# A two-layer hybrid encoder trunk on one Trainium2 core: the phases of a layer laid over one another at their borders, and the attention maximum taken from packed pairs of heads

## The chip, the core and the metric

The kernel runs on one core of one Trainium2 chip. The core has five engines with an instruction queue each: TensorE (PE in the profile, with its weight loads as PEld), VectorE (DVE), ScalarE (ACT), GpSimd (POOL) and SyncE (SP, which here only issues DMAs). Each works its queue in order, and they wait for one another through semaphores. The metric is the device time of one execution in microseconds (us). A kernel's time is the median of its runs; one more execution is taken with the hardware profiler, and its trace is what is read here.

## The reference

There are two layers over x of 1024 tokens by 1024 channels, all float32. In each layer one input projection feeds four token mixers: softmax attention with 8 query heads and 2 key heads of width 64; HGRN2, a gated linear recurrence of 4 heads with 128x128 states, run forward and backward; Mamba-2's SSD with 8 heads, also in both directions; and GLA, linear attention of 4 heads with a gate from a low-rank projection, in both directions. Each branch gets a SiLU gate, the four are joined and go through one output projection, and a LayerNorm ends the layer.

```
for i in range(DEPTH):
    h = einsum('bsd,dn->bsn', x, w_in[i])
    y_a = attention_branch(...)   # softmax(q k^T / 8) v, 128 queries at a time
    y_h = hgrn2_branch(...)       # S_t = diag(g_t) S_{t-1} + k_t v_t^T ; o_t = S_t^T q_t, both ways
    y_s = ssd_branch(...)         # conv, softplus time steps, h_t = exp(dt A) h_{t-1} + dt B x^T, both ways
    y_g = gla_branch(...)         # g = log_sigmoid(low @ w2 + b)/16, the same scan as HGRN2
    out = einsum('bsn,nd->bsd', concat(y_a, y_h, y_s, y_g), w_out[i])
    x = layer_norm(alpha * x + out)
```

"Time steps" and "gates" in the change's name are the softplus of SSD's `dt` and the log-sigmoid of GLA's low-rank projection. Both come from one narrow input tile, `sp`.

## The kernel before

**Tiles.** Activations lie transposed, channels on partitions and tokens along the free axis, in two halves of 512 tokens. Every input and output projection is computed to better than plain fp32r: activation and weight are split into a high and a low fp32r part, and three products are added, `xh*whi`, `xl*whi` and `xh*wlo`. One column tile of 128 output channels takes 48 matmuls of 128x512. ACT casts a weight tile to `whi`, POOL subtracts to get `wlo`. Results that a later phase needs go to DRAM scratch (`hdr`, `yd`) and come back by DMA.

**Phases.** Per layer: (1) q, k, v projections; (2) attention in 8 blocks of 128 queries; (3) HGRN2, head by head; (4) SSD in four tiles of two heads; (5) GLA in two pairs of heads (p = 0, 1), with the output projection beside it; (6) LayerNorm. In an attention block, `a_s` takes each query row's maximum over 1024 keys: per key group 4 matmul pairs into `S` (one head each, with the high and low halves of q stacked to 128 rows), each followed by one DVE reduction. `a_e` computes the transposed scores `ST` with the negative maximum folded in, ACT takes the exponential into `Pt`, and POOL adds up the eight `Pt` for the row sums (`psum`). `a_pv` multiplies by v into `O`, `Z` is the row sum over partitions. HGRN2 and GLA share `tree` (names `lv`, `QP`, `M`, `C`, `T`), which works through seven levels of a gated block decomposition, each with small matmuls on PE and four products on DVE; then come states (`kst`, `P`, `S`) and outputs (`ot`). In GLA `gss` is the sum of squares for the norm, one per output. In SSD, `sP` makes states, `yd` and `yo` the outputs, and DVE combines them (`u`, `ytmp`).

**What sets the order.** The instruction order of every engine is chosen when the program is built, by a planner. Mixer steps are generators, queued with `M(name, ..., needs, lane)` on twelve lanes; projections are generators too, queued with `F(name, ..., after)` as one list of fillers. A generator yields what its next piece waits for: tiles, free PSUM banks (`"A:1"`, `"P:1"`) or free buffers of the two large SBUF pools (`"k2:8"`: eight of 62 buffers of 128x512; `"k4:1"`: one of 8 of 128x1024). `run()` (line 548) keeps a clock for each engine from cost formulas (`Eng.call`, line 262) and always advances the lane whose wait is over first. If that lies more than 100 ns ahead, or if TensorE has fewer columns in the current tick of 3413 ns than `share` asks (`behind`, line 143; `KNOBS` holds the share, 0.5), it advances the filler. A table of dependencies at the end of `layer` (lines 1818 to 1895) fixes which phase may begin after which step: `sp` after HGRN2's last projection and `spp` (gates and time steps, `spec_post`) after its third head; HGRN2's first scan `hn0` after attention's last block; SSD's first group `sgp0` after HGRN2's last head `hm3`; GLA's first loads `gp0` after SSD's fourth tile `sm3`.

**Names the steps below touch.** `NP = (7, 8)` is how many `Pt` and `psum` tiles attention may have alive in each layer. `GL` is how many `k2` buffers have to be free before GLA loads. The SP queue carries every DMA, weights (`wraw`) and reloads alike, in the planner's order.

## Time and profile before

| | us |
|---|---|
| median of 3 runs (2638.04 to 2647.71) | 2640.66 |
| the profiled execution | 2644.85 |
| its span, first to last instruction | 2643.0 |
| PE busy in it | 2481.6 |
| DVE busy | 1588.1 |
| POOL busy | 1227.7 |
| ACT busy | 1092.9 |

The span is the time between the first and the last instruction. The 1.85 us between it and the execution's own time lie around it. "Busy" is the time in which an engine had at least one instruction running. PE's instructions overlap, so a busy PE may still be slowed: "PEclk" is the share of full clock that it was granted, and is 0.97 over the span. Almost all instructions stand under line 299, where a helper records them, so groups are told apart by the names of their tiles (`out<-in`). One fp32 matmul of the program stands in the profile as two records, one fp32r matmul as one.

### The profile page before, as it was taken

The page shows a single profiled execution, that of the slowest core. Times are in us where ns is not written, and L with a number is a line of the kernel's source. Part 1 is how long each engine was busy: PE and PEld are TensorE (multiplying, and loading weights), DVE is VectorE, ACT ScalarE, POOL GpSimd, SP SyncE. Part 2 cuts the span into 40 slices and gives each one's busy share as a digit, 9 for nine tenths or more (in the row PEclk, how much of TensorE's full clock was granted, in tenths as well). Part 3 has the DMA queues.
Part 4 walks back from the last instruction along what each step waited for, and adds up shares of the span by engine and source line. Part 5 has one row for each costly group of instructions (what it writes and reads, how often), then busy time and mean ns, then how long its engine had stood idle before and what let it go on. Part 6 is the DMA issues. An engine that isn't in the chain of part 4 may idle for free. (4 is left out here: it accounts for less than half of the span.)

```text
span 2643.0 us, 46508 instructions
## 1 busy us (share of the span) xinstructions
PE 2481.6 (94%) x18352; PEld 1855.2 (70%) x18352; DVE 1588.1 (60%) x2895; ACT 1092.9 (41%) x2100; POOL 1227.7 (46%) x932
## 2 busy tenths in 40 slices
PE   8999899999989997889989999999999999988996
PEld 6855457777877886667777655577777787866675
DVE  2574520565489778863555745206664898868737
ACT  4445453332464433334344444533334543433342
POOL 3556663223335446423554566642223454564334
PEclk9999999999989998989999999999999899999998
DMA  6311112011137447622343111120111365676232
GB/s 210 100 48 52 36 43 66 33 53 49 46 112 252 148 148 256 218 71 89 100 162 112 64 38 48 51 68 29 57 41 46 131 237 152 189 262 203 79 104 100
DMA packets 170173, 284.38 MB, mean 108 GB/s; under 512 B 17780, under 2 KB 43380, under 8 KB 169956
## 3 DMA queue, kind: packets, MB, share of 16 engines
q1 hardware_dynamic: 169956, 281.41, 32.5%
q8 instruction: 145, 2.38, 0.4%
q14 instruction: 72, 0.59, 0.1%
HBM read 205.39 MB, written 75.96 MB: 106 GB/s over the span
## 5 line engine op out<-in xcount | busy, mean ns | idle before, releaser
L299 POOL TENSOR_TENSOR wlo<-wraw,whi 128x512 fp32r<-128x512 f32 x372 | 509.9, 1391 | 585.3 <-ACT whi L299 528.7
L299 PE MATMUL proj<-xh,whi 128*128 128x512 f32 x1056 | 429.4, 407 | 4.7 <-DVE u L299 4.7
L299 PE MATMUL proj<-xl,whi 128*128 128x512 f32 x1056 | 415.1, 393 | 0.0
L299 PE MATMUL projh<-xh,whi 128*128 128x512 f32 x704 | 287.8, 409 | 10.4 <-ACT whi L299 9.6
L299 POOL TENSOR_TENSOR psum<-psum,Pt 128x1024 f32<-128x1024 f32 x96 | 228.6, 2381 | 128.2 <-ACT Pt L299 123.1
L299 ACT CAST whi<-wraw 128x512 fp32r<-128x512 f32 x372 | 216.6, 623 | 165.0 <-DMA wraw<-in_wt 63.7
L299 PE MATMUL proj<-xh,wlo 128*128 128x512 f32 x1056 | 281.0, 400 | 0.0
L299 PE MATMUL projh<-xl,whi 128*128 128x512 f32 x704 | 280.2, 398 | 0.3 <-DVE xl L299 0.3
L299 PEld LDWEIGHTS proj<-xh,whi 128*128 128x128 f32 x1056 | 199.6, 189 | 49.1 <-ACT ga L299 5.5
L299 PE MATMUL oproj<-mxh,whi 128*128 128x512 f32 x512 | 217.8, 425 | 15.9 <-ACT whi L299 9.2
L299 PEld LDWEIGHTS proj<-xl,whi 128*128 128x128 f32 x1056 | 200.2, 190 | 37.2
L299 PEld LDWEIGHTS proj<-xh,wlo 128*128 128x128 f32 x1056 | 192.6, 188 | 41.3 <-issue 2.1
L299 ACT ACTIVATE Pt<-ST 128x512 f32<-128x512 f32 x256 | 151.1, 597 | 135.6 <-PE ST L299 133.8
L299 PE MATMUL oproj<-mxl,whi 128*128 128x512 f32 x512 | 206.2, 403 | 0.0
L299 PE MATMUL projh<-xh,wlo 128*128 128x512 f32 x704 | 193.9, 398 | 0.0
L299 DVE TENSOR_REDUCE mx<-S 128x1 f32<-128x1024 f32 x128 | 151.9, 1218 | 53.5 <-PE S L299 52.4
L299 DVE TENSOR_TENSOR QP<-QP,T 128x512 f32<-128x512 f32 x168 | 144.7, 861 | 48.4 <-PE lv L299 47.5
L299 PEld LDWEIGHTS projh<-xh,whi 128*128 128x128 f32 x704 | 134.8, 192 | 54.9 <-issue 13.4
L299 ACT COPY M<-C 128x256 f32<-128x256 f32 x168 | 69.4, 415 | 241.2 <-DVE C L299 241.2
L299 PE MATMUL oproj<-mxh,wlo 128*128 128x512 f32 x512 | 152.7, 412 | 4.1 <-POOL wlo L299 4.1
L299 PEld LDWEIGHTS projh<-xl,whi 128*128 128x128 f32 x704 | 134.9, 192 | 27.5 <-DVE xl L299 1.5
L299 PEld LDWEIGHTS projh<-xh,wlo 128*128 128x128 f32 x704 | 129.0, 189 | 35.3 <-issue 9.7
(241 smaller groups left out, 4602.1 us busy)
## 6 DMA issues: line engine op xcount, KB each, us to landing
wraw<-in_wt SPq DMA_DIRECT2D x244, 256.0 KB
wraw<-in_wo SPq DMA_DIRECT2D x128, 256.0 KB
hdr<-zs SPq DMA_DIRECT2D x64, 256.0 KB
zs<-hdr SPq DMA_DIRECT2D x64, 256.0 KB
bc<-dr SPq DMA_DIRECT2D x64, 256.0 KB
yld<-yd SPq DMA_DIRECT2D x56, 256.0 KB
hdr<-sp SPq DMA_DIRECT2D x40, 256.0 KB
yd<-o SPq DMA_DIRECT2D x40, 256.0 KB
```

The lines of the kernel that those rows point to most:

```text
L299: return real(*args, **kw)
```

## The change

The dependency table and the planner's knobs change, and with them the order on every engine:

- **Gates and time steps first.** `sp` becomes a filler right after the q, k, v tiles, and `spp` needs only it (and twelve free `k2` buffers).
- **HGRN2's first head.** Its projection may start after attention's block 4 (`aP{H0}`, H0 = 4) in place of block 6, its scan no longer needs attention's end but two free `k4` buffers. From block 4 on attention may keep only NQ = 4 `Pt`/`psum` tiles alive.
- **SSD's and GLA's starts.** `sgp0` needs HGRN2's third head in place of its fourth; `sgp1` needs SSD's `sw1` in place of `sm0`, for which `CB` is kept apart from `Cc` and `Bt`. GLA's first loads need SSD's third tile (`sm2`) and the last input projection in place of the fourth tile; its second loads need `sm3`.
- **Knobs.** `share` goes from 0.5 to 1.0; POOL's cost formula is a little higher; `a_pv` gets a lane of its own.
- **Attention's maximum.** `a_qprep` also makes a copy `qp` of q with 64 channels a head, and transposes it so that one `Q2` chunk holds two heads on partitions 0 to 63 and 64 to 127. `a_s` then issues two matmuls of 64 rows, one per head, for one half of the keys, into the two halves of `S`. The reduction gives two columns at once, and one more DVE operation joins the two halves. As many matmuls and reductions are issued as before; per block there are 4 more transposes and 2 more ACT copies.
- **Row sums.** The additions into `psum` go from POOL to DVE.

```diff
+H0, NQ = 4, 4
-KNOBS = ((None, 100, 0.5),)
+KNOBS = ((None, 100, 1.0),)
-                cost = 155 + 2.09 * n + (120 if fn == "tensor_copy" else 0)
+                cost = 160 + 2.17 * n + (120 if fn == "tensor_copy" else 0)
@@ h_mix, second_half
+                yield ["k4:2"]
@@ spec_post
-            yield [spec, w2]
+            yield [spec, w2, "k2:12"]
@@ a_qprep
+                    qp = k2("qp", F32R)
+                    ac.copy(qp, qr)
+                    yield [qp, "A:1"]
+                    pt = transpose4(lambda c: qp[:, ck(c)], "qpT", F32R)
+                    Q2 = k2("Q2", F32R)
+                    ac.copy(Q2, pt.bitcast(F32))
@@ a_s
-                for c in range(4):
-                    yield [QT, "P:1"]
-                    S = bigps("S")
-                    for sh in range(2):
-                        mm(hs(S, sh), QT[:, ck(c)], KK[g * 2][sh], True, True)
-                    yield [S]
-                    ve.tensor_reduce(out=mx[:, c:c + 1], in_=S, axis=AX.X, op=ALU.max)
+                for c in range(2):
+                    for sh in range(2):
+                        yield [Q2, "P:1"]
+                        S = bigps("S")
+                        for e in range(2):
+                            r = slice(e * 64, e * 64 + 64)
+                            mm(hs(S, e), Q2[r, ck(2 * g + c)], KK[g * 2][sh][r], True, True)
+                        yield [S]
+                        ve.tensor_reduce(out=mx[:, sh * 4 + 2 * c:sh * 4 + 2 * c + 2], in_=AV(S, 0, [[HALF, 2], [1, HALF]]), axis=AX.X, op=ALU.max)
+                tt(ve, mx[:, 0:4], mx[:, 0:4], mx[:, 4:8], ALU.max)
@@ a_e
-                    yield [lambda: live[0] < NP[li], "k4:1"]
+                    yield [lambda: live[0] < (NP[li] if ti < H0 else NQ), "k4:1"]
-                        tt(gp, acc_s, acc_s, P, ALU.add)
+                        tt(ve, acc_s, acc_s, P, ALU.add)
@@ the table of dependencies
+        F(f"sp{li}", spec_proj, after=x1 + [f"set{li}"], ws=[wsrc("sp")])
+        M(f"spp{li}", spec_post, needs=[f"sp{li}"], lane=3)
-            F(f"hp{li}{h}", h_proj(h), after=... [f"set{li}", f"aP{li}6" if h == 0 else f"aP{li}7"],
+            F(f"hp{li}{h}", h_proj(h), after=... [f"set{li}", f"aP{li}{H0}" if h == 0 else f"aP{li}7"],
-            M(f"hn{li}{h}", a, needs=[f"hp{li}{h}", f"aP{li}7"])
+            M(f"hn{li}{h}", a, needs=[f"hp{li}{h}"])
-        F(f"sp{li}", spec_proj, after=[f"hp{li}3"], ws=[wsrc("sp")])
-        M(f"spp{li}", spec_post, needs=[f"sp{li}", f"hm{li}2"], lane=3)
-            M(f"sgp{li}{g}", ... (exps if g == 0 else [f"sm{li}0"]), lane=3)
+            M(f"sgp{li}{g}", ... ([f"hm{li}2"] if g == 0 else [f"sw{li}1"]), lane=3)
-            M(f"gp{li}{p}", g_load(p), needs=names + ([f"sm{li}3"] if p == 0 else [f"gn{li}0"]), lane=8)
+            M(f"gp{li}{p}", g_load(p), needs=names + ([xlast, f"sm{li}2"] if p == 0 else [f"sm{li}3"]), lane=8)
```

What the planner makes of it, at three places.

**PE, layer 0, about the third attention block.** `S` is the score tile for the maximum, `ST` the transposed scores, `projh` a filler projection. Before:

```order
L299 MATMUL S<-KK,QT 128x512 x2
L299 MATMUL ST<-QT,KK 128x512
L299 MATMUL ST<-QM,KK 128x512
L299 MATMUL S<-KK,QT 128x512 x2
L299 MATMUL qhT<-ident,qhl 128x128 x4
L299 MATMUL projh<-xh,whi 128x512
L299 MATMUL projh<-xl,whi 128x512
```

and now:

```order
L300 MATMUL S<-KK,Q_1949 128x512 x2
L300 MATMUL ST<-QT,KK 128x512
L300 MATMUL ST<-QM,KK 128x512
L300 MATMUL projh<-xh,whi 128x512
L300 MATMUL projh<-xl,whi 128x512
L300 MATMUL projh<-xh,wlo 128x512 x4
L300 MATMUL qpT<-ident,qp 128x128 x4
```

The `S` matmuls still come two by two, and full-size matmuls still stand on both sides of each pair; `S` now reads 64 rows in each, and `qpT`, the transposes of the packed q, are new.

**SP, layer 0, where the input projections end and the output projection begins.** `wraw<-in_wo` are the output projection's weights, `yld` its input, `M`, `q`, `T` and `V` GLA's first loads, `off` a load of SSD's fourth tile. Before:

```order
L299 DMA off<-dro 64x512 x4
L299 DMA hdr<-u 128x512
L299 DMA zs<-hdr 128x512
L299 DMA wraw<-in_wo 128x512 x2
L299 DMA xr<-in_xT 128x512 x2
L299 DMA wraw<-in_wo 128x512 x2
L299 DMA xr<-in_xT 128x512
L299 DMA hdr<-u 128x512
L299 DMA zs<-hdr 128x512
L299 DMA M<-hdr 128x512
L299 DMA q<-hdr 128x512
L299 DMA T_9326<-hdr 128x512 x2
```

and now:

```order
L300 DMA yld<-yd 128x512 x4
L300 DMA M<-hdr 128x512
L300 DMA q<-hdr 128x512
L300 DMA T_9169<-hdr 128x512 x2
L300 DMA wraw<-in_wo 128x512 x4
L300 DMA hdr<-zs 128x512 x2
L300 DMA off<-dro 64x512 x4
L300 DMA V<-hdr 128x512 x2
```

Before, GLA's first loads stood behind the first eight weight loads of the output projection. Now four of them stand ahead of its first weight load, and ahead of the fourth tile's last `off`. In layer 1 the first loads stand behind the weights as before.

**DVE, layer 0, the same border.** `QP<-q,T` is the first product of GLA's tree, `u` and `ytmp` are SSD's fourth tile, second half, `acc` the sums of the output projection. Before:

```order
L299 SCALAR_TENSOR_TENSOR S<-S,dec,sP 128x64 x6
L299 SCALAR_TENSOR_TENSOR acc<-xr,oproj 128x512 x2
L299 SCALAR_TENSOR_TENSOR u<-u,pk,yd 128x512
L299 TENSOR_TENSOR ytmp<-yo,off 128x512
L299 TENSOR_TENSOR ytmp<-yo,off 128x384
L299 SCALAR_TENSOR_TENSOR acc<-xr,oproj 128x512 x4
L299 TENSOR_TENSOR QP<-q,T_9352 128x1024
L299 TENSOR_TENSOR QP<-q,T_9326 128x1024
```

and now:

```order
L300 SCALAR_TENSOR_TENSOR S<-S,dec,sP 128x64 x6
L300 TENSOR_TENSOR QP<-q,T_9384 128x1024
L300 TENSOR_TENSOR QP<-q,T_9169 128x1024
L300 SCALAR_TENSOR_TENSOR acc<-xr,oproj 128x512 x2
L300 TENSOR_TENSOR near<-lv,imask 128x128 x2
L300 TENSOR_TENSOR M<-M,T_9384 128x128x2
L300 TENSOR_TENSOR QP<-QP,T_9384 128x256x2
L300 TENSOR_TENSOR C<-M,T_9384 128x128x2
L300 TENSOR_TENSOR T<-T_9384 128x512
L300 COPY_PREDICATED near<-masks,lv 128x128 x2
L300 SCALAR_TENSOR_TENSOR acc<-xr,oproj 128x512 x2
L300 SCALAR_TENSOR_TENSOR u<-u,pk,yd 128x512
```

GLA's tree now begins ahead of the fourth tile's last outputs, by one `u`, two `ytmp` and some `acc`.

Counted over the whole order of PE, as numbers of matmuls of the program:

| | before, layer 0 | before, layer 1 | now, layer 0 | now, layer 1 |
|---|---|---|---|---|
| projection matmuls between the first `S` and the last `Z` of attention | 368 | 410 | 490 | 500 |
| `oproj` matmuls between GLA's first `lv` and its last `gss` | 324 | 392 | 398 | 496 |
| `oproj` matmuls behind GLA's last `gss` | 358 | 242 | 304 | 200 |

The changes of tile form between neighbouring matmuls (full, 64 or 32 columns, 64 rows) number 663 before and 929 now. `gk` (16 matmuls a layer) and `colT` (16), which are the gates and time steps, stand beside HGRN2's last head and behind it before, and now beside attention's first two blocks. In layer 1 the first `proj` of HGRN2's first head stands behind the last `Z` of attention before and now; in layer 0 it stood behind it, and now stands ahead of it.

More of the change, by code (lines that the diff above doesn't have):

```diff
@@ L1265, in gen @@
                     yield None
-                sd["g", g] = (Cc, CB, Bt)
+                sd["g", g] = (Cc, Bt)
+                sd["cb", g] = CB
             return gen
@@ L1290, in gen @@
                 colA, dr = sd["colA"], sd["dr"]
-                CB = sd["g", n // 2][1]
+                CB = sd["cb", n // 2] if n % 2 == 0 else sd.pop(("cb", n // 2))
                 def rows(hf, e):
@@ L1336, in gen @@
                 colB, dro, dec = (sd[k] for k in ("colB", "dro", "dec"))
-                Cc, CB, Bt = sd["g", n // 2] if n % 2 == 0 else sd.pop(("g", n // 2))
-                del CB
+                Cc, Bt = sd["g", n // 2] if n % 2 == 0 else sd.pop(("g", n // 2))
                 X, xt = sd.pop(("x", n))
@@ L1582, in gen @@
                     tt(ve, q8, q8, AV(rq, 0, [[1, 8], [0, 64]]), ALU.mult)
+                    qp = k2("qp", F32R)
[4 more added lines that the diff above has]
+                    ac.copy(Q2, pt.bitcast(F32))
+                    del qp
                     for g in range(2):
@@ L1592, in gen @@
                         ac.copy(QT, pt.bitcast(F32))
-                        qts[ti, g] = (QT, qhl)
+                        qts[ti, g] = (QT, Q2, qhl)
             return gen
@@ L1600, in gen @@
                 yield [lambda: (ti, g) in qts]
-                QT, qhl = qts.pop((ti, g))
-                mx = mt("c8", [128, 4], name="mx")
-                for c in range(4):
-                    yield [QT, "P:1"]
-                    S = bigps("S")
-                    for sh in range(2):
-                        mm(hs(S, sh), QT[:, ck(c)], KK[g * 2][sh], True, True)
-                    yield [S]
-                    ve.tensor_reduce(out=mx[:, c:c + 1], in_=S, axis=AX.X, op=ALU.max)
-                    drop(S)
+                QT, Q2, qhl = qts.pop((ti, g))
+                mx = mt("c8", [128, 8], name="mx")
+                for c in range(2):
+                    for sh in range(2):
+                        yield [Q2, "P:1"]
[5 more added lines that the diff above has]
+                        ve.tensor_reduce(out=mx[:, sh * 4 + 2 * c:sh * 4 + 2 * c + 2], in_=AV(S, 0, [[HALF, 2], [1, HALF]]), axis=AX.X, op=ALU.max)
+                        drop(S)
+                del Q2
+                tt(ve, mx[:, 0:4], mx[:, 0:4], mx[:, 4:8], ALU.max)
+                mx = mx[:, 0:4]
                 mh = AV(qhl, 64, [[128, 4]])
@@ L1643, in gen @@
                         acc_s = k4("psum")
-                        tt(gp, acc_s, pts[ti, 0], P, ALU.add)
+                        tt(ve, acc_s, pts[ti, 0], P, ALU.add)
                         live[0] += 1
                     elif st:
-                        tt(gp, acc_s, acc_s, P, ALU.add)
+                        tt(ve, acc_s, acc_s, P, ALU.add)
                 sums[ti] = acc_s
@@ L1835, in layer @@
             M(f"ae{li}{ti}", a_e(ti), needs=[f"akv{li}a", f"akv{li}b"], lane=6)
[L1836 removed]
+            M(f"aP{li}{ti}", a_pv(ti), needs=[f"akv{li}a", f"akv{li}b", f"az{li}3"], lane=11)
         for h in range(4):
[L1839 removed]
+            F(f"hp{li}{h}", h_proj(h), after=[f"hm{li}{h - 2}"] if h > 1 else [f"set{li}", f"aP{li}{H0}" if h == 0 else f"aP{li}7"],
               ws=[wsrc("hi", h), wsrc("hf", h), wsrc("hb", h), wsrc("hq", h)])
             a, b = h_mix(h)
[L1842 removed]
+            M(f"hn{li}{h}", a, needs=[f"hp{li}{h}"])
             M(f"hm{li}{h}", b)
@@ L1860, in layer @@
         for g in range(2):
-            M(f"sgp{li}{g}", s_group_post(g), needs=[f"sB{li}{g}", f"sC{li}{g}"] + (exps if g == 0 else [f"sm{li}0"]), lane=3)
+            M(f"sgp{li}{g}", s_group_post(g), needs=[f"sB{li}{g}", f"sC{li}{g}"] + ([f"hm{li}2"] if g == 0 else [f"sw{li}1"]), lane=3)
             for n in (2 * g, 2 * g + 1):
```

2 lines of the change are left out of this document (removed).

## The prediction

> **What bounds the kernel now.** I read the page's busy shares and clock first, then the busy time of each engine stage by stage, then what PE waited for, and last single rows where the order changes.
>
> ```profile
> PE 2481.6 (94%) x18352; PEld 1855.2 (70%) x18352; DVE 1588.1 (60%) x2895; ACT 1092.9 (41%) x2100; POOL 1227.7 (46%) x932
> core 0: 2643.0 us, clock 0.970
> ```
>
> PE sets the time, but not fully: it sits idle for 2643.0 - 2481.6 = 161 us, and 3% of the clock is withheld, which is 0.03 x 2643 = 79 us of full-speed work. No order of the same matmuls can win more than these 240 us. The stages tell where they lie (window, length, then busy time and instructions of PE, PEld, DVE, ACT, POOL; then granted clock, DMA share, GB/s):
>
> ```profile
> 126.00:440.00 314.00, 294.36 (x1236) 174.15 (x1235) 144.13 (x164) 148.33 (x247) 184.70 (x95) 0.98 0.16 49
> 722.00:760.00 38.00, 31.34 (x256) 22.34 (x257) 30.95 (x43) 29.54 (x43) 14.48 (x11) 0.82 0.19 70
> 990.00:1190.00 200.00, 167.29 (x2370) 126.24 (x2372) 152.74 (x292) 68.16 (x131) 96.34 (x83) 0.87 0.55 182
> 1440.00:1755.00 315.00, 304.67 (x1320) 189.89 (x1320) 148.16 (x182) 153.43 (x259) 190.85 (x99) 0.98 0.17 54
> 2040.00:2075.00 35.00, 30.46 (x238) 20.96 (x237) 26.05 (x40) 28.13 (x42) 12.59 (x10) 0.80 0.20 76
> 2310.00:2560.00 250.00, 224.69 (x2749) 168.37 (x2748) 168.34 (x313) 90.42 (x168) 113.37 (x105) 0.95 0.50 164
> ```
>
> For each I add the idle time and the withheld clock (length times one less the clock). Attention, first and fourth row: 19.6 + 6.3 and 10.3 + 6.3, together 42.5 us. Gates and time steps, second and fifth row: 6.7 + 6.8 and 4.5 + 7.0, together 25 us. SSD's end with most of GLA, third and sixth row: 32.7 + 26.0 and 25.3 + 12.5, together 96.5 us. These three kinds of border hold 164 of the 240 us, and the change touches all three. The rest (start, LayerNorms, tail, HGRN2) it hardly touches.
>
> **Gates and time steps.** Their cost in place is seen on PE (start, duration, what; in brackets the idle time before and its releaser):
>
> ```profile
> 737.18 0.47 PE L299 MATMUL proj<-xh,whi 128*128 128x512 f32 x1 [2.76 <-DVE u L299]
> 746.90 0.76 PE L299 MATMUL gk<-low,w2h 32*128 32x512 f32 x1 [3.04 <-DVE near L299]
> ```
>
> The gate matmuls `gk` need DVE to free their banks, DVE is at HGRN2's scan and SSD's convolution `u`, and PE, which waits in order, lets its clock fall to 0.82 and 0.80. Moved to the layer's start, `spp` finds DVE emptier, 50 us of 126 in layer 0:
>
> ```profile
> 0.00:126.00 126.00, 115.92 (x523) 92.85 (x524) 50.08 (x128) 55.73 (x133) 56.44 (x56) 1.00 0.49 161
> ```
>
> It still waits for its own operands, and behind a waiting `gk` stand `projh` fillers and the first `S`. I let each layer give back one such wait of 3 us: 25 - 6 = **-19 us** (bounds: 0, if the whole stall moves along, and -25).
>
> **Attention: the packed maximum.** PE's pace is in three neighbouring starts, and the price of changing the tile form in the fourth:
>
> ```profile
> 726.37 1.98 PE L299 MATMUL proj<-xh,wlo 128*128 128x512 f32 x8
> 728.18 0.39 PE L299 MATMUL proj<-xh,whi 128*128 128x512 f32 x1
> ...
> 731.35 0.39 PE L299 MATMUL proj<-xh,whi 128*128 128x512 f32 x1
> 731.58 0.39 PE L299 MATMUL proj<-xl,whi 128*128 128x512 f32 x1
> 731.90 0.47 PE L299 MATMUL lv<-QP,M 128*32 128x32 f32 x32
> ```
>
> Eight matmuls take 728.18 - 726.37 = 1.81 us, so 0.227 us each. From the full `proj` to the 32-column `lv` it is 0.32 us, so a change of form costs 0.09 us. No 64-row matmul of 512 columns is in this trace. The nearest rows are the scan's, with half and with all the rows:
>
> ```profile
> L299 PE MATMUL S<-KK,QT 128*128 128x512 f32 x256 | 85.3, 415 | 1.7 <-ACT QT L299 1.7
> L299 PE MATMUL lv<-QP,M 128*64 128x64 f32 x512 | 21.9, 228 | 0.0
> L299 PE MATMUL lv<-QP,M 64*64 64x64 f32 x512 | 12.2, 230 | 5.2 <-DVE QP L299 3.8 <-ACT M L299 1.1 <-DVE near L299 0.4
> L299 PE MATMUL qhT<-ident,qhl 128*128 128x128 f32 x128 | 15.3, 242 | 1.6 <-DVE qhl L299 1.6
> ```
>
> 512 matmuls of 64 rows cost 12.2 us where 512 of 128 rows cost 21.9, so two row halves run side by side, nearly at twice the rate. I take the 256 `S` at half of 0.227: -29 us (bound on the other side: 0, side by side not at all). Against it stand the changes of form, 929 - 663 = 266, at 0.09: +24 us, because each pair of `S` still stands alone between full matmuls. The 64 new transposes, at 15.3 / 128 = 0.12, add 8 us. Net **+3 us** (bounds -21 without the drains, +32 without the packing). The Trainium skill, "TensorEngine Tiling (Array Packing)", section Tiling Modes, says that tiles work in parallel and that a change of tiling mode drains the engine. Its table's factor of two alone would make this part -21 us, and its drain, at this trace's 0.09 us, takes that back; the row agrees.
>
> **Attention: who adds the row sums, and what fills PE.**
>
> ```profile
> L299 POOL TENSOR_TENSOR psum<-psum,Pt 128x1024 f32<-128x1024 f32 x96 | 228.6, 2381 | 128.2 <-ACT Pt L299 123.1 <-PE S L299 4.4
> L299 POOL TENSOR_TENSOR psum<-Pt 128x1024 f32<-128x1024 f32 x16 | 38.0, 2377 | 23.5 <-ACT Pt L299 23.5
> L299 DVE TENSOR_TENSOR QP<-q,T x24: 1216/1222/2292, 472.4 to 2482.0; 128x1024 f32<-128x1024 f32 x24
> L299 DVE TENSOR_REDUCE mx<-S 128x1 f32<-128x1024 f32 x128 | 151.9, 1218 | 53.5 <-PE S L299 52.4
> ```
>
> POOL loses 267 us, 133 a layer of its 185 to 191 in attention; it was not the bound there, so that wins nothing by itself. DVE gains 112 additions, for which the nearest row is a product of the same size from SBUF to SBUF, 1.222 us alone and up to 2.29. With POOL nearly empty I take the median: 56 x 1.222 = 68 us a layer. DVE's 144 us of 314 become 212, 68%: covered, as long as the queue behind each addition can wait. That queue holds the `mx` reductions, which free the banks of the next `S` and lead to `QM` and so to `ST`. What fills PE is counted in the order: 122 and 90 more projection matmuls stand inside attention, 212 x 0.227 = 48 us of work, more than the 42.5 us that the stage has to give. If the stage kept its length, all 42.5 would be won. But the queue on DVE is longer now, `spp` shares the first block's ACT, DVE and `k2` buffers, and from block 4 on only four tiles may live. I take a third, **-14 us** (bounds: -42 and +26, if attention lengthens by half of DVE's new 137 us, less what is won). HGRN2's first head stands beside attention's end in layer 0 alone, and only by a few matmuls, so I give it no term of its own.
>
> **HGRN2 and SSD.** SSD's first group beside HGRN2's last head moves work between stages that have little to give:
>
> ```profile
> 440.00:722.00 282.00, 279.39 (x2846) 221.05 (x2845) 141.95 (x309) 96.34 (x205) 84.37 (x80) 1.00 0.14 46
> 760.00:990.00 230.00, 225.18 (x1241) 188.30 (x1238) 189.75 (x348) 94.85 (x180) 109.52 (x87) 0.99 0.54 177
> ```
>
> Idle there is 2.6 and 4.8 us. I put **0** (bounds +/-5).
>
> **GLA.** The scan is a chain over PE, DVE and ACT that PE's fillers, the output projection, have to cover:
>
> ```profile
> L299 PE MATMUL lv<-q,ks x256: 186/193/250, 1041.5 to 1171.0; 64*32 64x32 f32 x128
> L299 PE MATMUL gss<-sq,ones x16: 590/592/1220, 1131.6 to 1234.0; 128*128 128x512 f32 x16
> L299 PE MATMUL lv<-q,ks x256: 187/211/259, 2360.4 to 2486.2; 64*32 64x32 f32 x128
> L299 PE MATMUL gss<-sq,ones x16: 590/592/697, 2453.9 to 2556.3; 128*128 128x512 f32 x16
> ```
>
> From first `lv` to last `gss` it lasts 192.5 us in layer 0 and 195.9 in layer 1. Behind it nothing is left but dense `oproj`. The order now puts 398 in place of 324 `oproj` inside the chain, and 496 in place of 392. If the chain keeps its length, these 74 + 104 matmuls cost nothing there and are gone from what follows: 178 x 0.227 = **-40 us**. They would fill 40 of the 96.5 us that the stage has to give, which leaves room for the chain's own waits (bounds: 0, if each matmul put into the chain delays it by its own length, and -96). That the chain also begins earlier is small: on DVE it passes one `u`, two `ytmp` and some `acc`.
>
> The same move puts GLA's first four loads ahead of the output projection's first weights on SP, where PE already stood:
>
> ```profile
> 1000.10 2.10 SPq L299 DMA_DIRECT2D yld<-yd  x4
> 1002.25 1.57 SPq L299 DMA_DIRECT2D wraw<-in_wo  x3
> ...
> 1008.17 0.80 PE L299 MATMUL oproj<-mxh,whi 128*128 128x512 f32 x1 [9.22 <-ACT whi L299]
> ...
> 990.00:1056.00 66.00, 49.51 (x542) 40.06 (x541) 53.74 (x94) 23.70 (x47) 43.95 (x33) 0.87 0.80 255
> ```
>
> Four loads of 256 KB are 1 MB, 4 us at the 255 GB/s of that window, ahead of weights that PE waited 9.22 us for. Behind them wait the casts to `whi`, and with these PE's whole queue. I take **+3 us** (bounds 0 and +6; layer 1 keeps its order).
>
> **The sum.** -19 + 3 - 14 + 0 - 40 + 3 = -67 us. The profiled execution took 2644.85 us, 1.85 more than its span; it becomes 2578, with a span of 2576. It lies 4.2 us above the median of the runs, 2640.66, so the median becomes 2574 us.
>
> **The rivals.**
>
> (a) *PE stays dense through GLA and attention.* The new fillers end the idle time, so the clock is never withheld, and the chain, which ran partly at half clock, shortens too. For it: a clock of 0.87 in the third window means that its own small matmuls ran slow. Against it: DVE is busy 152.74 of 200 us there, so the chain cannot shrink much. Two thirds of the 164 us, less 3 + 3: -103, 2538 us.
>
> (b) *GLA's chain lengthens by what is put into it.* PE works in order, so a filler ahead of an `lv` delays it; the chain's DVE products then start later, and the 40 us come back as a longer chain. For it: `share` at 1.0 inserts fillers whether or not the chain's next step is ready. Against it: 58.7 and 37.8 us were lost in the stage without them. Then -27, 2614 us. The change would hardly do what it says at this border.
>
> (c) *Slower: DVE takes POOL's place as the one that is late in attention.* The place is DVE's queue between `psum` and `mx`. Each addition that `QM` has to wait behind lengthens the block by 1.222 us; if all 112 do, that is +137 us, and 137 - 67 = +70, 2711 us. It decides from the point where half of them (68 us) lie on the way to `ST`. For it: a block has 7 additions and 8 reductions in one queue. Against it: 68% busy is below what DVE carries in GLA. The Trainium skill, "GPSIMD Engine Reference", section Key points, says that GpSimd's SBUF interfaces are shared with VectorE, with contention where a DVE instruction has two SBUF inputs, as these additions have. The spread of the `QP` row, 1.222 to 2.292 us, is what one would expect of that; by the upper figure the additions would take 257 us.
>
> **How the numbers follow.** Forecast, -67 within 30 either way: 0.52. (a) 0.13, (b) 0.23, (c) 0.12. The forecast's own range is 2545 to 2605. To hold 8 of 10 the whole range reaches over (a), (b) and the lighter part of (c): 2520 to 2650. The time of this kernel spreads by about 0.4% between runs, so 0.5% (13 us) is about what can be told from no change. Faster by more than that: the forecast, (a) and most of (b), 0.83. Within it: the rest of (b) and a (c) that only takes the gain back, 0.08. Slower: the rest of (c), 0.09.
>
> **What would show it.** Right: PE's clock near 1.0 where `gk` and `colT` stand, at the layer's start, and no stall of 10 us behind HGRN2's last head; as many `oproj` behind the last `gss` as counted, with the time from first `lv` to last `gss` still 190 to 200 us; pairs of `S` that start within some 10 ns of each other, with 0.09 us lost on either side; DVE at about two thirds of attention, its `psum` near 1.2 us. Wrong: the time from first `lv` to last `gss` at 210 us or more (b); PE waits on `QM`, `ST` or `S` that end with DVE `mx` or `qhl` and add up to tens of us (c); the wait for the first `oproj` at 13 us or more in layer 0, which would double the last term.

## The result: slower by 1.2%, with PE busy longer and no less idle

The changed kernel takes 2673.9 us (median of 4 runs, 2672.1 to 2678.1) against 2641.2 us for the kernel before: 1.0123 of it, 95% interval 1.0100 to 1.0146. The forecast was 2574, and 2650 was the upper end of the range. The profiled execution took 2674.97 us. The page of the changed kernel, and its clock:

```profile
PE 2513.1 (94%) x18416; PEld 1833.5 (69%) x18416; DVE 1662.5 (62%) x3039; ACT 1101.1 (41%) x2128; POOL 960.5 (36%) x820
core 0: 2673.1 us, clock 0.970
```

PE is idle for 2673.1 - 2513.1 = 160 us where it was 161, and the clock is 0.970 as before. Not one of the 240 us that stood to be won is gone; the 30 us more of span are 31.5 us more of PE's busy time (2481.6 before). Since a busy PE may be one that fills or drains, I read the stages next. The stages' windows of the changed kernel are the time up to the first `S`, attention, and GLA from the first `oproj` to the last `gss`, for layer 0 and then layer 1 (window, length, busy time and instructions of PE, PEld, DVE, ACT, POOL, granted clock, DMA share, GB/s):

```profile
0.00:132.00 132.00, 118.84 (x508) 92.99 (x508) 48.35 (x119) 70.51 (x151) 61.58 (x60) 0.96 0.46 149
132.00:461.00 329.00, 320.77 (x1369) 178.30 (x1369) 219.02 (x275) 174.35 (x296) 66.15 (x48) 0.99 0.18 58
998.00:1244.00 246.00, 214.15 (x2634) 158.67 (x2635) 159.14 (x288) 83.09 (x155) 109.86 (x102) 0.88 0.45 146
1331.00:1466.00 135.00, 120.94 (x538) 95.97 (x538) 67.13 (x134) 74.52 (x158) 75.96 (x65) 0.95 0.40 133
1466.00:1806.00 340.00, 327.60 (x1382) 181.17 (x1382) 218.39 (x275) 173.31 (x295) 70.12 (x49) 0.98 0.18 58
2328.00:2593.00 265.00, 235.80 (x2818) 178.58 (x2816) 196.00 (x362) 95.28 (x182) 132.32 (x117) 0.95 0.50 162
```

and the same stages of the kernel before, cut at the same events:

```profile
0.00:113.00 113.00, 102.92 (x459) 82.23 (x460) 39.58 (x113) 51.68 (x126) 50.95 (x52) 1.00 0.53 172
113.00:416.00 303.00, 283.36 (x1194) 164.93 (x1193) 152.56 (x176) 143.64 (x241) 182.94 (x93) 0.98 0.15 46
1008.00:1235.00 227.00, 201.34 (x2595) 150.54 (x2596) 153.71 (x284) 80.73 (x151) 105.40 (x96) 0.90 0.47 155
1332.00:1444.00 112.00, 104.56 (x473) 84.47 (x473) 51.67 (x126) 53.70 (x129) 61.66 (x55) 0.95 0.47 155
1444.00:1740.00 296.00, 285.67 (x1235) 174.39 (x1234) 145.45 (x177) 145.34 (x245) 186.45 (x95) 0.98 0.16 51
2315.00:2557.00 242.00, 216.69 (x2696) 161.68 (x2696) 161.73 (x299) 88.09 (x165) 111.80 (x103) 0.95 0.50 165
```

Idle time and withheld clock (length times one less the clock) of a stage are called its loss from here on. Both layers together, before and now:

| stage | loss before | loss now | length before | length now |
|---|---|---|---|---|
| up to the first `S` | 10.1 + 13.0 = 23 | 18.4 + 20.8 = 39 | 225 | 267 |
| attention | 25.7 + 16.3 = 42 | 11.5 + 19.2 = 31 | 599 | 669 |
| GLA, first `oproj` to last `gss` | 48.4 + 37.4 = 86 | 61.4 + 42.5 = 104 | 469 | 511 |

Attention lost 11 us less, where 14 were forecast, but PE is busy 79 us longer in it. The start lost 16 more, and GLA, where 40 us were to be won, lost 18 more. All stages together lose 240 us before and now (161 + 79 and 160 + 80): what one stage won, others lost. What is left is PE's added busy time.

### The profile page after: what moved, and what is told of

The parts are those of the page before. It is cut to its first block, busy times and chain, and to the rows that moved or that the text cites. A ratio compares the mean times of both kernels' runs of the same rounds, so it can differ in the third digit from the quotient of the medians.

```text
span 2673.1 us, 46651 instructions
## 1 busy us (share of the span) xinstructions
PE 2513.1 (94%) x18416; PEld 1833.5 (69%) x18416; DVE 1662.5 (62%) x3039; ACT 1101.1 (41%) x2128; POOL 960.5 (36%) x820
## 5 line engine op out<-in xcount | busy, mean ns | idle before, releaser
L300 PE MATMUL projh<-xh,whi 128*128 128x512 f32 x704 | 294.1, 418 | 15.4 <-ACT whi L300 12.8
L300 PE MATMUL oproj<-mxh,whi 128*128 128x512 f32 x512 | 223.6, 437 | 20.2 <-ACT whi L300 14.9
L300 DVE TENSOR_TENSOR psum<-psum,Pt 128x1024 f32<-128x1024 f32 x96 | 120.4, 1255 | 89.5 <-ACT Pt L300 89.1
L300 DVE TENSOR_REDUCE mx<-S 128x2 f32<-128x1024 f32 x128 | 153.8, 1218 | 25.7 <-PE S L300 25.6
L300 PEld LDWEIGHTS projh<-xh,wlo 128*128 128x128 f32 x704 | 129.8, 191 | 42.5 <-issue 16.9
L300 PEld LDWEIGHTS lv<-QP,M 128*32 128x32 f32 (+2 forms) x6144 | 86.2, 119 | 105.7 <-issue 82.4
```

Source lines behind the costliest of these rows:

```text
L300: return real(*args, **kw)
```

## The experiments

Each kernel computes all of the reference. Names with u_ undo a part in the changed kernel, names with d_ do a part alone in the kernel before, names with o_ change numbers of the planner, in the kernel before or in one of the others. Ratios are to the kernel before, run beside on the same chip (its medians: 2636.7 to 2643.1). Differences between two changed kernels are of their times; by the ratios they come out up to 4 us higher or lower. A kernel whose change moves the order at all moves it everywhere; how much that matters is the last part, and a difference of some tens of us between two orders is not the price of the part that was undone.

### Undoing one part at a time

Packing undone (`u_pack`): `a_s` and the transposes of `Q2` as before.

```diff
-mm(hs(S, e), Q2[r, ck(2 * g + c)], KK[g * 2][sh][r], True, True)
+mm(hs(S, sh), QT[:, ck(c)], KK[g * 2][sh], True, True)
```

> The changed kernel with the packed maximum undone: one head per matmul of 128 rows, no copy qp and no transposes qpT; all else as changed. Theory D (drains): in attention the changed kernel's PE is busy 321 of 329 us and 328 of 340, and a packed pair of S costs 0.435 us to the next matmul plus 0.1 us at its entry, against 0.454 us for a full pair, so undoing wins 128 x 0.08 = 10 us and the 8 us of transposes: about -18, 2656 us. Rival V (the additions on DVE are what is late): nothing from this, 2674 within 6. Rival F (the loss is in GLA's chain): likewise 2674 within 6.

Measured: 2642.8 us, 1.0019 [1.0003, 1.0036], 31 us less than the changed kernel, 13 below theory D's figure. Nearly the whole loss goes when the packing goes; but the order is new too, and GLA's loss is 50 us here in place of 104. The packing's own price needs kernels of one order, and they come below.

The share put back (`u_share`):

```diff
-KNOBS = ((None, 100, 1.0),)
+KNOBS = ((None, 100, 0.5),)
```

> The changed kernel with the planner's share back at 0.5, all else as changed. Theory F: GLA's chain from first lv to last gss went from 193 and 197 us to 218 and 239 because share 1.0 puts fillers ahead of steps that are ready; with 0.5 it falls back to about 200 in both layers, and 20 to 30 us come back: 2648 us. Theory D: nothing in GLA depends on it, the filler only moves; 2674 within 8. Rival G (GLA's early start against SSD's last tile is what lengthens it): chain stays above 215 in both layers, 2674 within 8.

Measured: 2683.3 us, 1.0166 [1.0132, 1.0201], 9 us more than the changed kernel and just above the band of theories D and G. The chain stayed long, 217.8 and 244.2 us: `share` is not what lengthens it.

The row sums back on POOL (`u_adds`):

```diff
-tt(ve, acc_s, acc_s, P, ALU.add)
+tt(gp, acc_s, acc_s, P, ALU.add)
```

> The changed kernel with the row sums added on POOL again, all else as changed. Rival V: DVE's 219 us of 329 in attention fall to 150 and -20 us or more come back: 2654 or less. Theory D: PE is dense in attention and waits for DVE under 1 us there, so nothing: 2674 within 8, or some us more because POOL's 2.38 us additions delay wlo. Theory F: 2674 within 8.

Measured: 2688.2 us, 1.0192 [1.0154, 1.0230], 14 us more than the changed kernel. Rival (c) falls, by the groups of the changed kernel: a `psum` addition takes 1.255 us, near the 1.222 that was forecast, DVE is busy 219.02 of 329 us, 67%, and all the `S` together waited 1.0 us for DVE's `mx`. That the additions help on DVE is not shown: 14 us is less than a new order alone can make.

```profile
L300 DVE TENSOR_TENSOR psum<-psum,Pt 128x1024 f32<-128x1024 f32 x96 | 120.4, 1255 | 89.5 <-ACT Pt L300 89.1
L300 DVE TENSOR_REDUCE mx<-S 128x2 f32<-128x1024 f32 x128 | 153.8, 1218 | 25.7 <-PE S L300 25.6
L300 PE MATMUL S<-KK,Q 64*128 64x512 f32 x256 | 64.2, 499 | 1.0 <-DVE mx L300 1.0
```

GLA's loads released as before (`u_gload`):

```diff
-[xlast, f"sm{li}2"] if p == 0 else [f"sm{li}3"]
+[f"sm{li}3"] if p == 0 else [f"gn{li}0"]
```

> The changed kernel with GLA's loads released as before (first pair after SSD's fourth tile, second pair after the first pair's second half), all else as changed. Rival G: GLA's tree and SSD's fourth tile contend for DVE and for the k2 buffers, so the chain falls back to about 200 us; it starts some 10 us later, so net -10 to -20: 2655 to 2664. Theory F: the chain keeps 215 us or more since the fillers stay between its steps, and starts later: 2674 to 2685. Theory D: no say, 2674 within 8.

Measured: 2694.7 us, 1.0217 [1.0179, 1.0256], 21 us more than the changed kernel, above the bands of all three theories. Whether the earlier loads help is read at their place. The first `oproj` of layer 0 waits 2.52 us for its weights in the changed kernel, not 9.22 and more, and 0.81 us in `u_gload`:

```profile
997.88 0.80 PE L300 MATMUL oproj<-mxh,whi 128*128 128x512 f32 x1 [2.52 <-ACT whi L300]
```

```profile
998.54 0.79 PE L300 MATMUL oproj<-mxh,whi 128*128 128x512 f32 x1 [0.81 <-ACT whi L300]
```

So the early loads did not shorten this wait; with them it is 1.7 us longer, as far as one place in two orders can tell. The 21 us lie elsewhere, and no run parts them from the new order.

This run also bears on the chain. First `lv` and last `gss` of GLA in layer 1, and SSD's fourth-tile products on DVE in that time, in the changed kernel:

```profile
L300 PE MATMUL lv<-q,ks x256: 186/193/215, 2354.8 to 2520.1; 64*32 64x32 f32 x128
...
L300 PE MATMUL gss<-sq,ones x16: 590/592/697, 2483.0 to 2592.8; 128*128 128x512 f32 x16
...
L300 DVE TENSOR_SCALAR Wm<-CB,colA x12: 272/279/1310, 2359.2 to 2404.1; 128x128 f32<-128x128 f32 x12
L300 DVE SCALAR_TENSOR_TENSOR Wm<-CB,colA,Wm x12: 350/352/1280, 2359.5 to 2405.4; 128x128 f32<-128x128 f32 x12
```

and in `u_gload`:

```profile
L300 PE MATMUL lv<-q,ks x256: 187/193/213, 2412.2 to 2548.9; 64*32 64x32 f32 x128
...
L300 PE MATMUL gss<-sq,ones x16: 591/593/1220, 2508.8 to 2616.6; 128*128 128x512 f32 x16
```

with this stage window:

```profile
2331.00:2617.00 286.00, 248.76 (x2848) 185.30 (x2846) 188.27 (x367) 98.29 (x191) 133.41 (x120) 0.93 0.48 153
```

The chain takes 238 us with SSD's `Wm` inside it and 205 in `u_gload`, where none lies inside, but the way from the first `oproj` to the last `gss` is 286 us in place of 265. A longer chain that starts earlier is no loss by itself; the length of the chain, which I had named as the sign, does not tell the time.

### What the packing costs, with the order held fixed

Three kernels have the same instructions in the same order (PE's 18416 records follow one another alike in all three), and differ in the operands of the 256 `S` matmuls alone. `u_side` uses two row halves, as the change does (only the first `S` of a pair reads `QT`); `u_seq` uses one row half for both; `u_full` uses all 128 rows.

```diff
 u_side: mm(hs(S, e), QT[0:64, ck(2*c)] if e == 0 else Q2[64:128, ck(2*g + c)], KK[g*2][sh][e*64:e*64 + 64], True, True)
 u_seq:  mm(hs(S, e), QT[0:64, ck(2*c + e)], KK[g*2][sh][0:64], True, True)
 u_full: mm(hs(S, e), QT[:, ck(2*c + e)], KK[g*2][sh], True, True)
```

Not shown: all three wait for `QT` too, and give the pair one cost in the planner, so that the order stays.

> The changed kernel, with one operand taken from another tile: the first of each pair of S reads rows 0 to 63 of QT (they hold the same high part of q as Q2), the second still rows 64 to 127 of Q2. The pair still lies on two row halves. This is the base of two other runs that have its order word for word. All theories: the changed kernel's 2674 us, within 10 (waiting for QT moves some instructions).

> As u_side in every instruction and its order, but both S of a pair use the same row half (rows 0 to 63 of QT and KK), so that they cannot run side by side; the form changes stay. If the halves of a pair really run side by side: 128 pairs x 0.227 us = +29 us against u_side, a little less where PE stood idle (+20 to +29). If they did not run side by side in the changed kernel (the packing itself fails): u_side +0 to +5.

> As u_side in every instruction and its order, but each S of a pair uses all 128 rows (QT against KK), so that no pair changes the form of the tile; the transposes, copies and the extra maximum stay. The pair then costs 2 x 0.227 = 0.454 us with no drain. Theory D (a pair between full matmuls drains the array twice, 0.10 us in and about 0.20 out, so 0.53 in all): u_side -10 us (-4 to -16). The forecast's drain of 0.09 each way (0.41 a pair): u_side +6. Drains cost nothing and the transposes and copies are the loss: u_side +25 to +29.

Measured: `u_side` 2663.3 us, 1.0087 [1.0066, 1.0107]; `u_seq` 2698.0, 1.0216 [1.0195, 1.0237]; `u_full` 2649.1, 1.0034 [1.0019, 1.0048]. `u_side` was to take what the changed kernel takes, 2673.9; its other operand changed the order, and with that alone it takes 11 us less. The first line of each page, in this order:

```profile
PE 2508.9 (94%) x18416; PEld 1828.2 (69%) x18416; DVE 1669.3 (63%) x3039; ACT 1103.8 (41%) x2130; POOL 971.1 (36%) x820
```

```profile
PE 2545.2 (94%) x18416; PEld 1848.5 (69%) x18416; DVE 1669.5 (62%) x3039; ACT 1105.3 (41%) x2130; POOL 968.4 (36%) x820
```

```profile
PE 2485.8 (94%) x18416; PEld 1852.1 (70%) x18416; DVE 1667.8 (63%) x3039; ACT 1104.3 (42%) x2130; POOL 965.1 (37%) x820
```

The halves do run side by side: on one row half the pairs cost 34.7 us more, 34.7 / 128 = 0.27 us each, where 0.227 is one matmul. Yet a pair of full matmuls is cheaper than a packed pair: 14.2 us less, 0.11 us a pair, and 23.1 us less of PE's busy time, 0.18 a pair. (The busy times are of single executions, 2668.9 and 2641.1 us, the slowest of `u_side` and the fastest of `u_full`; of the two figures the time is the safer.) With 2 x 0.227 = 0.454 for the full pair, the packed one takes 0.57 to 0.63 us, of which only 0.227 is work. The remaining 0.34 to 0.40 us are the two changes of form around it. Two pairs in the changed kernel's timeline (start, duration, what):

```profile
321.65 0.40 PE L300 MATMUL projh<-xl,whi 128*128 128x512 f32 x1
321.98 0.50 PE L300 MATMUL S<-KK,Q 64*128 64x512 f32 x2
322.41 0.53 PE L300 MATMUL qhT<-ident,qhl 128*128 128x128 f32 x4
322.87 0.49 PE L300 MATMUL S<-KK,Q 64*128 64x512 f32 x2
323.30 0.51 PE L300 MATMUL projh<-xh,whi 128*128 128x512 f32 x1
323.64 0.40 PE L300 MATMUL projh<-xl,whi 128*128 128x512 f32 x1
323.88 0.40 PE L300 MATMUL ST<-QT,KK 128*128 128x512 f32 x1
```

Into the pair it is 0.33 - 0.227 = 0.10 us, which the forecast had from `proj` to `lv` (0.09). From the pair to what follows it is 0.43 - 0.227 = 0.20 us. And the first full matmul behind a pair takes 0.34 us to the next in place of 0.227, another 0.11. Wherever full matmuls of 512 columns stand beside the pairs, the medians are 0.33, 0.43 and 0.34 us; in `u_full` the full matmul ahead of a pair and the one behind it take 0.23 us each to the next. The sum is 0.41 us a pair, at the upper end of what the comparison gives.

How the 0.20 in the middle divides, `u_seq` shows. There the two `S` of a pair run one after the other, and the pair's row lasts 0.73 us, where one matmul's lasts 0.39 to 0.40 without a change:

```profile
329.82 0.73 PE L303 MATMUL S<-KK,QT 64*128 64x512 f32 x2
330.48 0.50 PE L303 MATMUL ST<-QT,KK 128*128 128x512 f32 x1
330.82 0.40 PE L303 MATMUL ST<-QM,KK 128*128 128x512 f32 x1
```

So the second `S` starts about 0.34 us behind the first, 0.11 more than 0.227, and `ST` 0.32 behind the second, 0.10 more. A change of form thus costs about 0.10 us ahead of the first matmul of the new form and about 0.11 behind it, 0.2 in all, and the way out costs as much as the way in. The forecast's 0.09 was the first half alone. The second half stood in the kernel before as well, behind the 64-column matmuls of `O`, where the first full matmul takes 0.34 us to the next:

```profile
149.88 1.08 PE L299 MATMUL O<-Pt,Vt 128*64 128x512 f32 x4
150.89 0.50 PE L299 MATMUL ST<-QT,KK 128*128 128x512 f32 x1
151.23 0.40 PE L299 MATMUL ST<-QM,KK 128*128 128x512 f32 x1
151.47 0.40 PE L299 MATMUL projh<-xh,whi 128*128 128x512 f32 x1
```

Packing alone in the kernel before (`d_pack`), the reverse of `u_pack`'s edit:

> The kernel before with the packed maximum alone (the transposes of Q2, the pairs on two row halves, the maximum over two halves). Forecast: +3 us, 2641. Theory D (drains, transposes): +15 to +31 us, 2653 to 2669. If the loss of 31 us seen when it is undone in the changed kernel needs the changed order around it (the adds on DVE, the filled attention): 0 to +8.

Measured: 2660.8 us, 1.0075 [1.0054, 1.0095], 21 us more. The parts make about as much: 14 for the pairs by `u_full`, and 8 for the 64 transposes by the prediction's term, which no run isolates. The order is new here too, so that the two agree may be chance.

### The other parts alone, and together

Gates and time steps alone (`d_spec`):

```diff
+F(f"sp{li}", spec_proj, after=x1 + [f"set{li}"], ws=[wsrc("sp")])
+M(f"spp{li}", spec_post, needs=[f"sp{li}"], lane=3)
-F(f"sp{li}", spec_proj, after=[f"hp{li}3"], ws=[wsrc("sp")])
-M(f"spp{li}", spec_post, needs=[f"sp{li}", f"hm{li}2"], lane=3)
```

Not shown: `spec_post` also waits for twelve free `k2` buffers.

> The kernel before with the gates and time steps alone moved to the layer's start. Forecast: -19 us, 2620. Theory M (the stall moves along: gk and colT wait at the layer's start for DVE and ACT, which serve the first attention block there): 2633 to 2645, with the idle time and withheld clock behind HGRN2's last head gone (about 12 us a layer) and 8 to 12 us a layer more ahead of the first S or in attention.

Measured: 2700.7 us, 1.0243 [1.0213, 1.0274], 64 us more than before: no theory had that.

Attention's part alone (`d_att`): the sums on DVE, lane 11 for `aP`, H0 and NQ, `hp0` after block 4, and POOL's costs.

> The kernel before with attention's part alone: the row sums on DVE, aP in a lane of its own, four live tiles from block 4 on, HGRN2's first heads released earlier, POOL's costs. Forecast's term: -14 us, 2625. Theory that the attention's border had no loss that these edits reach (PE's idle time there is made of its drains, which stay): 2634 to 2646. Rival (c), DVE late: above 2660.

Measured: 2696.6 us, 1.0245 [1.0199, 1.0291], 60 us more, though attention itself lost about what it had (44 us, against 42) and became shorter (296 and 283 us). The time is in the band given for rival (c), but not for its reason: no matmul of `S` waited for DVE's `mx` there, and what grew is GLA's loss, 113 us against 86.

GLA's part alone (`d_gla`): share 1.0, GLA's loads, `sgp0` and `sgp1` with `CB` apart, POOL's costs.

> The kernel before with GLA's part alone: share 1.0, GLA's loads released earlier, SSD's group steps released earlier (CB kept apart), POOL's costs. The order has 430 and 480 oproj inside the chain in place of 324 and 392. Forecast: -40 + 3, 2602. Rival (b), the chain lengthens by what is put into it: 2628 to 2642, with first lv to last gss at 215 to 235 us in both layers.

Measured: 2687.1 us, 1.0191 [1.0161, 1.0222], 50 us more, far above both forecasts; the chain lasts 225 and 240 us.

Attention's and GLA's parts together, without packing and moved gates (`u_packspec`):

> The changed kernel without the packed maximum and without the moved gates (attention's and GLA's parts together). Forecast's terms: -14 - 40 + 3, 2589. If the terms of the runs so far add up: 2643 (packing undone alone) less what moving the gates costs there; theory M gives 2637 to 2649. The order has 446 and 384 oproj inside the chain, against 398 and 496 in the changed kernel, and 348 and 338 projection matmuls in attention against 490 and 500.

Measured: 2633.4 us, 0.9991 [0.9972, 1.0011]: no gain, where -51 was forecast. Parts that cost 60 and 50 us alone cost nothing together. All four parts alone add up to 21 + 64 + 60 + 50 = 195 us (POOL's cost formula is in two of them); the change, which is all of them, costs 33. The terms don't add.

`u_packspec` beside `u_pack` also gives the moved gates' own price where the packing is away: 2642.8 - 2633.4 = +9 us (ratios 1.0019 and 0.9991; their intervals overlap a little and the orders differ, so the size is not sure). Three stages of each layer are the start, attention, and the scan of HGRN2's last head, from its first `lv` to its last, where `gk` stood before; first `u_packspec`, with the gates in their old place:

```profile
0.00:118.00 118.00, 107.47 (x482) 86.48 (x483) 43.12 (x113) 52.72 (x127) 54.17 (x54) 1.00 0.49 164
1312.00:1429.00 117.00, 105.19 (x474) 85.14 (x475) 58.44 (x129) 55.03 (x132) 67.07 (x58) 0.94 0.46 150
118.00:413.00 295.00, 279.83 (x1175) 161.15 (x1174) 189.82 (x231) 143.25 (x240) 49.78 (x35) 0.98 0.16 49
1429.00:1711.00 282.00, 271.54 (x1164) 158.48 (x1163) 186.99 (x230) 139.36 (x237) 50.59 (x37) 0.99 0.15 46
679.00:745.00 66.00, 60.84 (x645) 44.34 (x633) 52.33 (x91) 42.34 (x66) 25.89 (x21) 0.95 0.15 53
1984.00:2053.00 69.00, 64.58 (x662) 45.77 (x662) 55.49 (x91) 43.73 (x69) 27.33 (x22) 0.90 0.16 57
```

and `u_pack`, with the gates first:

```profile
0.00:129.00 129.00, 115.07 (x488) 89.76 (x488) 46.94 (x118) 68.83 (x148) 58.09 (x58) 0.96 0.45 147
1312.00:1451.00 139.00, 122.74 (x536) 97.47 (x536) 63.73 (x134) 73.77 (x157) 77.01 (x66) 0.94 0.39 131
129.00:437.00 308.00, 289.68 (x1238) 169.89 (x1236) 211.59 (x256) 162.69 (x272) 66.23 (x44) 0.99 0.17 56
1451.00:1761.00 310.00, 295.53 (x1250) 174.04 (x1250) 211.77 (x255) 159.63 (x270) 65.60 (x44) 0.98 0.17 55
705.00:768.00 63.00, 59.55 (x665) 45.53 (x667) 53.11 (x90) 19.16 (x36) 14.15 (x13) 0.97 0.26 88
2018.00:2082.00 64.00, 59.86 (x669) 45.89 (x668) 53.88 (x91) 20.05 (x37) 14.32 (x13) 1.00 0.28 88
```

In the last head's scan the loss falls from 19.8 to 9.5 us, both layers together: about half of it was not the gates' and stays. (From the kernel before to the changed one it falls from 25.5 to 12.3.) At the start the loss rises from 29.4 to 43.7, and in attention from 34.4 to 42.1. The part of the stall that left with the gates came back there, and grew.

### The order alone

The three parts alone have one thing in common: the planner puts every later instruction into a new order. Six kernels change nothing but its numbers. `d_pool` has POOL's new cost formula, `o_hi` slack 60 and share 0.8, `o_lo` slack 200, `o_mid` slack 200 and share 0.8, these four with the instructions of the kernel before. `o_best` is `u_packspec` with slack 200 and share 0.5, `o_gates` is `u_pack` with slack 200 and share 0.8.

```diff
 d_pool: -155 + 2.09 * n   +160 + 2.17 * n
 o_hi:   -KNOBS = ((None, 100, 0.5),)   +KNOBS = ((None, 60, 0.8),)
 o_lo:   -KNOBS = ((None, 100, 0.5),)   +KNOBS = ((None, 200, 0.5),)
 o_mid:  -KNOBS = ((None, 100, 0.5),)   +KNOBS = ((None, 200, 0.8),)
```

> The kernel before, with POOL's costs in the planner at 160 + 2.17 n for 155 + 2.09 n and nothing else: the same instructions, in another order. In it 182 and 110 output projections stand ahead of GLA's chain (before: 86 and 134) and 478 and 418 projections in attention (368 and 410). Theory O (the order alone sets the time; what is spent ahead of the chain or beside attention is missing later): +20 to +50 us, 2657 to 2687. Theory E (the edits' own work costs the time): 2638 within 6.

> The kernel before with the planner's slack at 60 and share at 0.8: the same instructions, in an order with many output projections ahead of GLA's chain, 320 and 158, and 464 and 436 projections in attention. Theory O: +50 to +80 us, 2688 to 2718. Theory E: 2638 within 13.

> The kernel before with the planner's slack at 200: the same instructions, in an order with nearly no output projection ahead of GLA's chain, 0 and 14, and few projections in attention, 266 and 264. Theory O: at or below the kernel before, 2600 to 2642, with less loss in GLA than before and more in attention. Theory E: 2638 within 13. Above 2655 both fall.

> The changed kernel without packing and without the moved gates, with slack 200 and share 0.5: 38 and 80 output projections ahead of GLA's chain, 274 and 238 projections in attention (with slack 100 and share 1.0: 38 and 38, 348 and 338, which took 2633). Theory O: 2605 to 2640. Theory E: 2633 within 13.

> The kernel before with the planner's slack at 200 and share at 0.8: the same instructions, 0 and 40 output projections ahead of GLA's chain, 424 and 414 inside it. If the two counts together tell a good order: 2615 to 2645, with 20 to 30 us lost in each chain (gaps and withheld clock). If the counts in GLA do not tell it: 2655 to 2690, like the three other new orders of these instructions.

> The changed kernel without packing alone (gates moved), with slack 200 and share 0.8: 26 and 54 output projections ahead of the chain, 434 and 368 inside it, 312 and 360 projections in attention. If the two counts tell a good order: 2620 to 2645 (with slack 100, share 1.0 it took 2643). If they do not: 2655 to 2690.

The table has the output projections ahead of GLA's chain and inside it as counted in each order (layer 0 / layer 1), GLA's loss from the stage windows (first `oproj` or first `lv`, whichever comes first, to last `gss`, both layers together), and the time.

| kernel | ahead | inside | GLA's loss, us | time, us | ratio |
|---|---|---|---|---|---|
| before | 86 / 134 | 324 / 392 | 86 | 2641.2 | |
| o_mid | 0 / 40 | 424 / 414 | 65 | 2636.5 | 0.9983 [0.9964, 1.0001] |
| o_lo | 0 / 14 | 304 / 386 | 102 | 2671.1 | 1.0108 [1.0083, 1.0134] |
| d_pool | 182 / 110 | 404 / 314 | 107 | 2673.5 | 1.0117 [1.0085, 1.0148] |
| o_hi | 320 / 158 | 264 / 436 | 138 | 2696.0 | 1.0202 [1.0177, 1.0227] |
| d_gla | 162 / 110 | 430 / 480 | 120 | 2687.1 | as above |
| d_att | 296 / 46 | 290 / 448 | 113 | 2696.6 | as above |
| d_spec | 226 / 242 | 360 / 344 | 132 | 2700.7 | as above |
| u_packspec | 38 / 38 | 446 / 384 | 76 | 2633.4 | as above |
| o_best | 38 / 80 | 380 / 374 | 51 | 2642.0 | 0.9997 [0.9985, 1.0009] |
| o_gates | 26 / 54 | 434 / 368 | 64 | 2653.7 | 1.0051 [1.0031, 1.0071] |
| u_pack | 34 / 46 | 436 / 424 | 50 | 2642.8 | as above |
| u_side | 38 / 72 | 456 / 422 | 61 | 2663.3 | as above |
| the change | 66 / 72 | 398 / 496 | 104 | 2673.9 | 1.0123 [1.0100, 1.0146] |

The same instructions in four other orders take from 5 us less to 53 us more. `d_pool`, which was to be nothing but a price in a table, costs 30 us. In the upper eight rows, all with PE's work as before, time goes up with GLA's loss, though not in step (`d_att` takes as long as `o_hi` with 25 us less of it): 65 us at the one end and 132 to 138 at the other, 2636 and 2696 to 2701. In the lower rows it does not: `o_best` has the least loss but one and is no faster than `u_packspec`. The last two rows differ in one operand and the order that came of it. GLA's loss is 43 us apart, the time 11: `u_side` loses 63 us in attention, where the change loses 31. GLA in the worst and the best of the four, first layer 0 of `o_hi`:

```profile
979.00:1289.00 310.00, 257.39 (x2893) 195.16 (x2892) 215.45 (x431) 102.83 (x200) 142.79 (x128) 0.91 0.46 146
```

and layer 0 of `o_mid`:

```profile
1002.00:1209.00 207.00, 187.02 (x2559) 139.46 (x2560) 146.63 (x263) 79.14 (x146) 93.89 (x88) 0.95 0.50 163
```

80 us are lost in the one and 30 in the other. In `o_hi`, 320 output projections are spent before the chain starts and 264 stand inside it. The output projection is a fixed stock of 768 matmuls a layer, and what is put at one place is missing at another.

How far the two counts carry: `d_pool` and `o_hi` came out as expected, `o_lo` did not (few ahead, but 304 inside, with a loss of 57 us in layer 0), `o_best` missed its band by 2 us, and "few ahead and enough inside" then had `o_mid` right and `o_gates` above the band for a good order, just below that for a bad one. The loss in GLA of `o_gates` is that of `o_mid`; the 17 us between them lie outside GLA. So the counts say something of GLA's loss; a rule for the whole time they are not. No kernel here is shown to be faster than the one before: the best ratio's interval reaches from 0.9964 to 1.0001.

## Why the prediction was wrong

By the prediction's own steps, 100 us off:

- **The packed maximum, +3: measured +14 for the pairs in one order, to which the prediction's 8 us for the transposes come; +21 alone in a new order.** The mechanism was right in both its halves (side by side, and drained), the price of a change of form wrong. "A change of form costs 0.09 us" was read from the last full matmul to the first of the new form. The first matmul of the new form then takes 0.11 us longer to the next, so a change costs about 0.2. The 256 changes around the 128 pairs cost 44 to 51 us by the comparison with `u_full`, 128 x 0.41 = 52 by the timeline, where 0.09 each gave 24, and outweigh the 29 us won. The Trainium skill, "TensorEngine Tiling (Array Packing)", section Tiling Modes, says that a change of mode drains the engine; the runs agree, and give the price that it leaves open.
- **The gates, -19: measured about +9.** Two steps failed. The 25 us lost where `gk` stood were all put down to the gates; without them the last head's scan still lost 12 us in the changed kernel. And "I let each layer give back one such wait of 3 us" was too little: the start and attention gave back 22 us in `u_pack`, more than the 10 us won at the old place. The bound of 0, that the whole stall moves along, was nearer than my value, and it was no bound.
- **Attention, -14.** Its loss fell by 11 us, and rival (c) fell, with the row that I had named. That the number came near is luck in part: `u_side`, with the same work in another order, lost 63 us in attention, 21 more than the kernel before. And the 48 us of projections put there came from later places, and I had asked only what they fill.
- **GLA, -40: its loss rose by 18 us.** "If the chain keeps its length" did not hold (218 and 238 us, past the 210 that I had set as the sign of rival (b)). Rival (b)'s cause, fillers put in ahead of an `lv`, is not borne out either: with `share` back at 0.5 the chain stayed as long. In layer 1, SSD's fourth tile lies inside it. The step that failed is the one ahead of these: 178 more `oproj` inside the chain were counted as 178 x 0.227 us gone from elsewhere. Moving matmuls of a fixed stock wins only what idle time they end, and idle time in this stage did not fall. The 18 us themselves belong to this order: `u_side` lost 61 us in the stage, less than the 86 before.
- **HGRN2 and SSD, 0.** No run isolates it.
- **GLA's loads, +3.** The wait for the first `oproj` did not grow but became 2.52 us. With the loads late it is 0.81, so the early loads cost 1.7 us there, inside the term's bounds. That undoing them costs 21 us in all has another cause, which no run isolates.
- **The sum.** Attention's and GLA's parts together were to bring -51 and brought -3, which is no change (`u_packspec`). The idle time and withheld clock that were to shrink by 19 + 14 + 40 us are 240 us before and now, and the packing's extra time on PE is not made good. The step behind all terms, that they may be added, failed: any of them reorders everything after it, which alone moved the time by -5 to +53 us. The kernel before has one of the better orders, and a change has to make good first what the new order loses. I had read PE's idle time as room; it was what was left after orders like these.

What stays open is what makes one order of the same instructions lose 65 us in GLA and another 138. The two counts may be a part of it; they are not all.

## What to carry to other kernels

A packed pair of matmuls standing alone between full ones pays for two changes of form, here 0.34 to 0.41 us together, and wins one matmul of 0.227: pack only runs that are long enough, and read the price of a change to the second matmul behind it, on the way in and on the way out. Where a planner sets the order, first time a few orders of the unchanged instructions; an edit whose expected gain is smaller than their spread can't be judged from its own cost. Work moved to cover a stall is taken from the place that it covered: the windows of both places belong in the sum.

## What the runs showed of the hardware

A change between full matmuls and 64-row ones costs about 0.2 us either way, about 0.10 ahead of the first matmul of the new form and 0.11 between it and the next (changed kernel and `u_seq`). So two full matmuls of 512 columns are faster than two half ones side by side that stand alone between full ones: 0.454 us against 0.57 to 0.63. The two row halves do run side by side, to the full within the noise: on one half, the same pairs cost 0.27 us more each, by the time, where one matmul is 0.227.
